# The memory tokens in four pieces, scaled by VectorE in the first layer

## The chip, the cores and the metric

The kernel runs on one core of one Trainium2 chip. The metric is the time of one execution in microseconds (us) of device time, the median of several runs. A profiled execution gives the trace from which rows are shown: PE is TensorE's matmul, PEld its weight load, DVE is VectorE, ACT ScalarE, POOL GpSimd, SP the engine that issues most copies; SPq, DVEq and so on are the engines' own instruction queues.

## The reference

The reference is a two-layer decoder trunk over 1024 tokens of width 1024 in float32. Each layer has a token mixer (a gated convolution in the first, attention with forget gates in the second), a cross-attention into 256 memory tokens with 4 heads, and a squared-ReLU MLP. What matters here is the memory side:

```
def memory_cross_attention(h, mem_n, w_q, w_k, w_v, w_o):
    q = (h @ w_q).reshape(B, S, MEM_HEADS, MEM_HEAD_DIM)
    k = (mem_n @ w_k).reshape(B, MEM_LEN, MEM_HEADS, MEM_HEAD_DIM)
    v = (mem_n @ w_v).reshape(B, MEM_LEN, MEM_HEADS, MEM_HEAD_DIM)
    ...
mem_n = rmsnorm(mem, norm_memsrc_g[l])
```

and the start of the convolution: `u = h @ w_pw1 + b_pw1`, with h = rmsnorm(x), then `a * sigmoid(gate)`, a depthwise convolution over 31 taps, and a layernorm over the width.

## The kernel before

The memory side is prepared ahead of its use. `memory_matrices`, a generator that is advanced a step at a time, multiplies wq with the keys and the values with wo, head by head, and stores the products (mqk, mvo) for later. It runs woven into `conv_layer`: a step for each half of x that is loaded, one behind each half that is normalized, two for each of the eight channel chunks of the convolution. A scheduler turns what the code issues into one fixed order for each engine; an engine takes its instructions in that order, and waits at one until what it needs is there. Instructions issued inside `tc.high_priority(offset=SMALL_FIRST)` are drawn forward in it.

The memory tokens lie in HBM with the width on partitions: `memT` is 128 x 8 chunks x 256 tokens, 1 MB. The steps of the first layer are these. One copy loads all of `mem`. ScalarE squares the eight chunks (L183 and L186, helper `sum_of_squares`), VectorE adds the squares (L187) into `acc`. TensorE multiplies `acc` with a column of 1/1024 (L162), VectorE adds epsilon (L210), GpSimd raises to the power -0.5 (L214), and TensorE spreads the result over the partitions (L171); VectorE keeps it as `mem_rs` (L483). ScalarE scales each chunk in place by the column `src0` of the gain (L471). The products of `mem` with two pieces of wk (tiles `praw`, 512 KB each, three buffers, L460) go into one PSUM bank of two halves of 8 products each (L276, helper `product`); VectorE multiplies that with `mem_rs` to get `kt` (L486). Products with two pieces of wv follow, copied out as `vt` by ScalarE (L488), then those of `kt` with wq, evacuated by ScalarE in quarters `o` (L503), then those of wo with `vt` (L521).

On the convolution's side the order is: `x` loaded in two halves of eight tiles of 256 KB (L135); squares of x, sums and inverse RMS by the same helpers; `h` (L225, VectorE), its high part (L229, ScalarE's cast) and low part (L149, VectorE), which together are `op`; the first gate weights split in the same way into `wh` (L152) and `wl` (L149); three products for each pair of parts (`op` with `wl`, and twice with `wh`); `u` (L390, VectorE); then the 49 instructions of VectorE per chunk that make the convolution (L413 to L428) and the sum `acc` for the layernorm (L361).

A product of two float32 operands stands in the trace as two MATMUL records, one of fp32r operands as one.

Of the kernel before, what the change touches and what calls it, by code (L numbers as in the profile page):

```python
# [12 lines left out]
F32 = mybir.dt.float32  # L13
F32R = mybir.dt.float32r
AF = mybir.ActivationFunctionType
ALU = mybir.AluOpType
# [3 lines left out]
P = 128  # L20
D = 1024
S = 1024
NCH = D // P
HALF = 512
MEM = 256
# [7 lines left out]
SMALL_FIRST = 4000  # L33
# [23 lines left out]
RMS_EPS = 1e-6  # L57
# [30 lines left out]
def trunk(ctx, tc, a, out):  # L88
    nc = tc.nc
    act, dve, pool, pe = nc.scalar, nc.vector, nc.gpsimd, nc.tensor  # L90
# [14 lines left out]
    def col(name, i):  # L105
        return par[:, COLS[name] + i : COLS[name] + i + 1]
# [31 lines left out]
    nrm = ctx.enter_context(tc.tile_pool(name="nrm", bufs=2))  # L138
# [3 lines left out]
    def bank(p):  # L142
        return p.tile([P, HALF], F32, name="mm", tag="mm")
# [11 lines left out]
    def token_mean(*accs):  # L155

        nb = accs[0].shape[-1] // P
        t = bank(ps)
        means = [t[:, i * nb : (i + 1) * nb] for i in range(len(accs))]
        for m, acc in zip(means, accs):  # L160
            for b in range(nb):
                pe.matmul(m[:, b : b + 1], acc[:, b * P : (b + 1) * P], mean_col, start=True, stop=True)  # L162
        return means

    def spread(v):

        nb = v.shape[-1]
        r = bank(ps)
        with tc.high_priority(offset=SMALL_FIRST):
            for b in range(nb):  # L170
                pe.matmul(  # L171
                    r[:, b * P : (b + 1) * P], v[:, b : b + 1].to_broadcast([P, P]), ident,
                    start=True, stop=True,
                )
        return r[:, : nb * P]

    def sum_of_squares(chunks):

        n = chunks[0].shape[-1]
        acc = nrm.tile([P, HALF], F32, name="acc", tag="t", bufs=4)[:, :n]  # L180
        for c, ch in enumerate(chunks):
            if c == 0:
                act.activation(acc, ch, AF.Square)  # L183
            else:
                sq = nrm.tile([P, HALF], F32, name="t", tag="t", bufs=4)[:, :n]
                act.activation(sq, ch, AF.Square)  # L186
                dve.tensor_tensor(acc, acc, sq, op=ALU.add)  # L187
        return acc
# [10 lines left out]
    def inverse_rms(chunks, eps):  # L199

        acc = sum_of_squares(chunks)
        with tc.high_priority(offset=SMALL_FIRST):
            return rms_of_sums([acc], eps)

    def rms_of_sums(accs, eps, name="r"):

        m, *rest = token_mean(*accs)
        nb = m.shape[-1]
        v = nrm.tile([P, 4], F32, name="v")[:, :nb]
        dve.tensor_scalar(v, m, eps, None, op0=ALU.add)  # L210
        for x in rest:
            dve.tensor_tensor(v, x, v, op=ALU.add)
        r = nrm.tile([P, 4], F32, name=name)[:, :nb]
        pool.tensor_tensor(r, v, mhalf[:, :nb], op=ALU.pow)  # L214
        return r
# [57 lines left out]
    def product(out_ps, terms):  # L273
        terms = [p for t in terms for p in passes(*t)]
        for i, (x, y) in enumerate(terms):
            pe.matmul(out_ps, x, y, start=i == 0, stop=i == len(terms) - 1)  # L276
# [176 lines left out]
    def memory_matrices(pp, pq, layer):  # L453

        wq, wk, wv, wo = (a[f"mem_{n}{layer}"] for n in ("wq", "wk", "wv", "wo"))
        ad, vd = mats[layer]

        def get(src):
            raw = pp.tile([P, NCH, P], F32, name="praw", bufs=3)
            nc.sync.dma_start(raw, src)  # L460
            return raw

        mem = pp.tile([P, NCH, MEM], F32, name="mem", bufs=1)
        nc.sync.dma_start(mem, a["memT"])
        if layer == 0:
            r = inverse_rms([mem[:, c, :] for c in range(NCH)], RMS_EPS)
            rt = const.tile([P, MEM // P], F32, name="mem_r")
            rs = const.tile([P, MEM], F32, name="mem_rs")
            mem_r.extend((rt, rs))
        for c in range(NCH):  # L470
            act.activation(mem[:, c, :], mem[:, c, :], AF.Copy, scale=col(f"src{layer}", c))  # L471
        for h in range(MEM_HEADS):
            kv = []
            for w, n in ((wk, "kt"), (wv, "vt")):
                t = bank(pq).rearrange("p (c m) -> p c m", c=2)
                for c in range(2):
                    x = get(w[2 * h + c])
                    product(t[:, c, :], [((x[:, k, :],), (mem[:, k, :],)) for k in range(NCH)])
                o = pp.tile([P, 2, MEM], F32, name=n, bufs=1)
                if w is wk:  # L480
                    if layer == h == 0:
                        dve.tensor_copy(rt, r)
                        dve.tensor_copy(rs, spread(r))  # L483
                    rb = mem_r[1].unsqueeze(1).to_broadcast([P, 2, MEM])
                    with tc.high_priority(offset=SMALL_FIRST):
                        dve.tensor_tensor(o, t, rb, op=ALU.mult)  # L486
                else:
                    act.copy(o, t)  # L488
                kv.append(o)
                yield  # L490
            kt, vt = kv
            for j in range(2):

                x = get(wq[h, j])
                for g in range(2):
                    t = bank(pq).rearrange("p (f m) -> p f m", f=2)
                    o = pp.tile([P, 4, P], F32, name="o").rearrange("p (f b) n -> p f (b n)", f=2)
                    for f in range(2):
                        product(t[:, f, :], [
                            ((x[:, 4 * c + 2 * g + f, :],), (kt[:, c, :],)) for c in range(2)  # L500
                        ])
                        gain = col(f"mem{layer}", 4 * j + 2 * g + f)
                        act.activation(o[:, f, :], t[:, f, :], AF.Copy, scale=gain)  # L503
                    nc.sync.dma_start(
                        ad[:, 4 * j + 2 * g : 4 * j + 2 * g + 2, h * MEM : (h + 1) * MEM], o
                    )
            yield
            for j in range(2):

                x = get(wo[h, j])  # L510
                for mc in range(2):
                    t = bank(pq)
                    product(t, [
                        (
                            (vt[:, c, mc * P : (mc + 1) * P],),
                            (x[:, 4 * c : 4 * c + 4, :].rearrange("p b n -> p (b n)"),),
                        )
                        for c in range(2)
                    ])
                    o = pp.tile([P, 4, P], F32, name="o")  # L520
                    act.activation(  # L521
                        o, t.rearrange("p (b n) -> p b n", b=4), AF.Copy,
                        scale=mem_r[0][:, mc : mc + 1],
                    )
                    nc.sync.dma_start(
                        vd[4 * j : 4 * j + 4, :, 2 * h + mc, :].rearrange("b p n -> p b n"), o
                    )
            yield
# [907 lines left out]
    with prep_pools(4) as pools, banks(2) as pm:  # L1436
        conv_layer(pm, chain(*(memory_matrices(*pools, l) for l in range(2))))
    sums = mem_attention(0)
# [90 lines left out]
```

## Time and profile before

| | us |
|---|---|
| median of 3 runs | 2794.61 |
| lowest, highest | 2787.88, 2794.71 |
| profiled execution | 2793.35 |
| its span, first to last instruction | 2791.6 |
| TensorE busy in it | 2722.8 |
| VectorE busy | 2019.9 |
| ScalarE busy | 1275.8 |

The span is the time between the first and the last instruction in the trace; the time of the same execution has 1.75 us around it. A row of a trace gives start, busy time, engine, line, operation, output and input tiles, shape and count of like instructions that follow each other; in brackets the idle time ahead and what ended it.

### The profile page before, as it was taken

What the parts mean: (1) busy time and instruction counts of PE and PEld (TensorE: products, weight loads), DVE (VectorE), ACT (ScalarE), POOL (GpSimd) and SP (SyncE); (2) the same over time, 40 slices, a digit from 0 to 9 for tenths busy, and PEclk for the clock granted to TensorE, in tenths of its full rate; (3) what the DMA queues carried; (4) which work ended last, traced back from release to release, by engine and by line L of the source; (5) the groups of instructions that cost most, each with busy time, mean ns of one, the idle gap of its engine ahead of it and who ended that gap; (6) DMA issues with size and microseconds to landing.
All of it is one profiled execution on the core that took longest, in us unless ns stands there. A gap on an engine that the chain in (4) does not pass through costs nothing. (4 is left out here: it accounts for less than half of the span.)

```text
span 2791.6 us, 35871 instructions
## 1 busy us (share of the span) xinstructions
PE 2722.8 (98%) x12840; PEld 2248.9 (81%) x12840; DVE 2019.9 (72%) x3118; ACT 1275.8 (46%) x2297; POOL 726.2 (26%) x489
## 2 busy tenths in 40 slices
PE   8999999999999999999999999999999999999998
PEld 6777777888888878888688888878888888878886
DVE  5999985555776667788787777775545866677886
ACT  5112134433365553334466666663423655543332
POOL 0000000000065633786000000000000365615773
PEclk9999999999999999999999999999999999999999
DMA  6334364420255576553222322244222355565651
GB/s 221 121 121 136 107 198 153 132 92 28 100 210 196 177 268 220 210 196 128 84 88 92 93 79 87 80 136 152 87 79 99 136 196 192 186 248 199 230 203 61
DMA packets 173426, 406.45 MB, mean 146 GB/s; under 512 B 18480, under 2 KB 47536, under 8 KB 172992
## 3 DMA queue, kind: packets, MB, share of 16 engines
q1 hardware_dynamic: 172992, 404.10, 42.8%
q8 instruction: 101, 1.65, 0.3%
q14 instruction: 77, 0.63, 0.1%
q10 hardware_dynamic: 256, 0.07, 0.0%
HBM read 280.75 MB, written 119.14 MB: 143 GB/s over the span
## 5 line engine op out<-in xcount | busy, mean ns | idle before, releaser
L1091 PE MATMUL mm<-op,w 128*128 128x512 f32 x5424 | 1237.6, 390 | 11.4 <-ACT m L975 8.3
L1091 PEld LDWEIGHTS mm<-op,w 128*128 128x128 f32 x5424 | 1020.3, 188 | 225.5 <-ACT m L975 9.2
L276 PE MATMUL mm<-op,wh 128*128 128x512 f32 x1056 | 329.3, 393 | 4.0 <-DVE op L149 3.9
L149 DVE TENSOR_TENSOR w<-r,w 128x512 fp32r<-128x512 f32 x264 | 275.0, 1045 | 32.7 <-ACT w L673 18.5
L673 ACT CAST w<-r 128x512 fp32r<-128x512 f32 x264 | 163.4, 622 | 265.4 <-PE mm L1091 237.7
L276 PEld LDWEIGHTS mm<-op,wh 128*128 128x128 f32 x1056 | 198.8, 189 | 49.2 <-DVE op L149 8.0
L1336 PE MATMUL mm<-op,wh 128*128 128x512 f32 x736 | 230.5, 394 | 0.0
L149 DVE TENSOR_TENSOR w<-t,w 128x512 fp32r<-128x512 f32 x180 | 196.5, 1106 | 31.9 <-ACT w L673 31.9
L276 PE MATMUL mm<-op,wl 128*128 128x512 f32 x528 | 209.8, 398 | 3.4 <-DVE wl L149 1.8
L667 POOL TENSOR_TENSOR t<-r,t 128x512 f32<-128x512 f32 x104 | 172.9, 1663 | 85.9 <-DVE w L149 81.6
L885 POOL TENSOR_TENSOR x<-x,x 128x512 f32<-128x512 f32 x112 | 165.0, 1496 | 112.5 <-ACT x L898 101.6
L214 POOL TENSOR_TENSOR r<-v,mhalf 128x4 f32<-128x4 f32 (+1 forms) x15 | 16.8, 1117 | 676.4 <-DVE v L210 665.4
L152 ACT CAST wh<-raw 128x1024 fp32r<-128x1024 f32 x96 | 100.7, 1050 | 194.9 <-PE mm L276 96.4
L673 ACT CAST w<-t 128x512 fp32r<-128x512 f32 x180 | 112.0, 622 | 153.8 <-PE mm L1091 118.0
L152 ACT CAST pth<-mm 128x512 fp32r<-128x512 f32 (+1 forms) x224 | 105.9, 496 | 149.4 <-PE mm L576 81.0
L987 DVE TENSOR_TENSOR x<-mm,x 128x512 f32<-128x512 f32 x160 | 109.3, 683 | 81.4 <-PE mm L1091 52.4
L1336 PEld LDWEIGHTS mm<-op,wh 128*128 128x128 f32 x736 | 138.6, 188 | 26.6
L1336 PE MATMUL mm<-op,wl 128*128 128x512 f32 x368 | 155.1, 421 | 2.9 <-DVE wl L149 1.9
L276 PE MATMUL mm<-op,xsh 128*128 128x512 f32 x512 | 157.8, 393 | 0.0
L428 DVE SCALAR_TENSOR_TENSOR x<-d,par,x 128x512 f32<-128x512 f32 x232 | 154.6, 745 | 0.0
L667 POOL TENSOR_TENSOR t<-r,r 128x512 f32<-128x512 f32 x52 | 80.0, 1539 | 280.2 <-DMA r<-in_ff_w 194.1
L149 DVE TENSOR_TENSOR wl<-raw,wh 128x1024 fp32r<-128x1024 f32 x96 | 116.7, 1222 | 38.2 <-ACT wh L152 36.4
(191 smaller groups left out, 4577.6 us busy)
## 6 DMA issues: line engine op xcount, KB each, us to landing
r<-in_ff_w SPq DMA_DIRECT2D x128, 512.0 KB, 4.1
op<-ua SPq DMA_DIRECT2D x80, 512.0 KB, 6.9
us<-x SPq DMA_DIRECT2D x128, 256.0 KB, 4.0
op<-us SPq DMA_DIRECT2D x64, 512.0 KB, 5.6
raw<-mvo SPq DMA_DIRECT2D x32, 512.0 KB, 3.3
ua<-ul SPq DMA_DIRECT2D x64, 256.0 KB, 2.7
ua<-uh SPq DMA_DIRECT2D x60, 256.0 KB, 2.7
raw<-in_pw SPq DMA_DIRECT2D x24, 512.0 KB, 5.1
```

Source lines behind the costliest of these rows:

```text
L149: dve.tensor_tensor(lo, src, hi.bitcast(F32), op=ALU.subtract)
L152: act.copy(hi, src)
L214: pool.tensor_tensor(r, v, mhalf[:, :nb], op=ALU.pow)
L276: pe.matmul(out_ps, x, y, start=i == 0, stop=i == len(terms) - 1)
L428: dve.scalar_tensor_tensor(out[s], d[:, j : j + n], w, y, op0=ALU.mult, op1=ALU.add)
L667: (dve if g in (2, 3, UP, UP + 1) else pool).tensor_tensor(t, raws[g, x], raws[g, y], op=ALU.subtract)
L673: act.copy(highs[n][0], raws[steps[n][:2]])
L885: eng.tensor_tensor(u[g, x], y1, y2, op=op_)
L987: dve.tensor_tensor(v, sums[key], v, op=ALU.add)
L1091: pe.matmul(sums[key], y, z, start=first and i == 0, stop=n == last_of[key] and i == len(terms) - 1, skip_group_check=True,)
L1336: pe.matmul(t, x, y, start=n == 0, stop=n == len(terms) - 1)
```

## The change

In the first layer `mem` is loaded by four copies of two chunks each, and the two pieces of wk are asked for among them: the first behind the first quarter, the second behind the last. ScalarE takes the eight squares alone. VectorE multiplies each chunk with its gain, in place, once ScalarE has squared it, and adds its square. The mean and the power are the same calls as before. In the second layer all stays as it was.

```
         mem = pp.tile([P, NCH, MEM], F32, name="mem", bufs=1)
-        nc.sync.dma_start(mem, a["memT"])
+        loaded_first = deque()
         if layer == 0:
-            r = inverse_rms([mem[:, c, :] for c in range(NCH)], RMS_EPS)
+
+            nc.sync.dma_start(mem[:, :2, :], a["memT"][:, :2, :])
+            loaded_first.append(get(wk[0]))
+            for c in range(2, NCH, 2):
+                nc.sync.dma_start(mem[:, c : c + 2, :], a["memT"][:, c : c + 2, :])
+            loaded_first.append(get(wk[1]))
+            sums = nrm.tile([P, HALF], F32, name="acc", tag="t", bufs=4)[:, :MEM]
+            for c in range(NCH):
+                sq = nrm.tile([P, HALF], F32, name="t", tag="t", bufs=4)[:, :MEM] if c else sums
+                act.activation(sq, mem[:, c, :], AF.Square)
+                dve.tensor_scalar(mem[:, c, :], mem[:, c, :], col("src0", c), None, op0=ALU.mult)
+                if c:
+                    dve.tensor_tensor(sums, sums, sq, op=ALU.add)
+            with tc.high_priority(offset=SMALL_FIRST):
+                r = rms_of_sums([sums], RMS_EPS)
             rt = const.tile([P, MEM // P], F32, name="mem_r")
             rs = const.tile([P, MEM], F32, name="mem_rs")
             mem_r.extend((rt, rs))
-        for c in range(NCH):
-            act.activation(mem[:, c, :], mem[:, c, :], AF.Copy, scale=col(f"src{layer}", c))
+        else:
+            nc.sync.dma_start(mem, a["memT"])
+            for c in range(NCH):
+                act.activation(mem[:, c, :], mem[:, c, :], AF.Copy, scale=col(f"src{layer}", c))
...
-                    x = get(w[2 * h + c])
+                    x = loaded_first.popleft() if loaded_first else get(w[2 * h + c])
```

The scheduler's order changes with it on every engine but GpSimd, from the start to the products of the first half of h with the first gate weights; from there on it is that of before. Three places are shown.

VectorE, from the first instruction that touches the memory tokens to the first low parts of h's work; before:

```order
L187 TENSOR_TENSOR acc<-acc,t 128x256 x7
L210 TENSOR_SCALAR v<-mm 128x2
L482 COPY mem_r<-r 128x2
L483 COPY mem_rs<-mm 128x256
L187 TENSOR_TENSOR acc<-acc,t 128x512 x7
L486 TENSOR_TENSOR kt<-mm,mem_rs 128x512
L210 TENSOR_SCALAR v<-mm 128x4
```

The same place of the change, from the last of the seven pairs of scale and add on:

```order
L476 TENSOR_SCALAR mem<-mem,par 128x256
L478 TENSOR_TENSOR acc<-acc,t 128x256
L210 TENSOR_SCALAR v<-mm 128x2
L498 COPY mem_r<-r 128x2
L499 COPY mem_rs<-mm 128x256
L187 TENSOR_TENSOR acc<-acc,t 128x512 x6
L502 TENSOR_TENSOR kt<-mm,mem_rs 128x512
L187 TENSOR_TENSOR acc<-acc,t 128x512
L210 TENSOR_SCALAR v<-mm 128x4
```

Seven adds have become eight scales and seven adds, and `kt` has moved ahead of the last add for the first half of x.

TensorE, from its first product to the products with the first gate weights; before:

```order
L276 MATMUL mm<-mem,praw 128x256 x2
L162 MATMUL mm<-mean_col,acc 128x1 x2
L276 MATMUL mm<-mem,praw 128x256
L171 MATMUL mm<-ident,r 128x128 x2
L276 MATMUL mm<-mem,praw 128x256 x14
L162 MATMUL mm<-mean_col,acc 128x1 x4
L276 MATMUL mm<-mem,praw 128x256 x2
L171 MATMUL mm<-ident,r 128x128 x4
L276 MATMUL mm<-mem,praw 128x256 x13
L276 MATMUL mm<-kt,praw 128x256 x12
L276 MATMUL mm<-op,wl 128x512
L276 MATMUL mm<-op,wh 128x512 x2
```

The same stretch of the change:

```order
L276 MATMUL mm<-mem,praw 128x256 x5
L162 MATMUL mm<-mean_col,acc 128x1 x2
L276 MATMUL mm<-mem,praw 128x256
L171 MATMUL mm<-ident,r 128x128 x2
L276 MATMUL mm<-mem,praw 128x256 x11
L162 MATMUL mm<-mean_col,acc 128x1 x4
L276 MATMUL mm<-mem,praw 128x256
L171 MATMUL mm<-ident,r 128x128 x4
L276 MATMUL mm<-mem,praw 128x256 x14
L276 MATMUL mm<-op,wl 128x512
L276 MATMUL mm<-op,wh 128x512
L276 MATMUL mm<-kt,praw 128x256 x12
```

Five products instead of two stand ahead of the mean of the memory tokens' squares, one instead of two between the mean and the spread for x, and a product of `op` with `wl` and one with `wh` have moved ahead of the products with `kt`.

ScalarE, from the casts of the first half of h to the first evacuations `o` of the products with `kt`; before:

```order
L229 CAST op<-h 128x512 x5
L488 COPY vt<-mm 128x512
L152 CAST wh<-raw 128x1024 x2
L229 CAST op<-h 128x512 x2
L503 ACTIVATE o<-mm,par 128x256 x2
L183 ACTIVATE acc<-x_78 128x512
```

The same place of the change:

```order
L229 CAST op<-h 128x512 x5
L504 COPY vt<-mm 128x512
L229 CAST op<-h 128x512
L152 CAST wh<-raw 128x1024
L229 CAST op<-h 128x512
L152 CAST wh<-raw 128x1024
L183 ACTIVATE acc<-x_78 128x512
L229 CAST op<-h 128x512
L186 ACTIVATE t<-x_80 128x512
L186 ACTIVATE t<-x_82 128x512
L186 ACTIVATE t<-x_84 128x512
L519 ACTIVATE o<-mm,par 128x256
```

A cast of h has moved between `vt` and the first `wh`, and the first evacuation `o` behind four squares of the second half of x.

## Rows read from the trace of the kernel before

**Rows 1.** The page: span, and busy time of the engines with their shares and numbers of instructions.

```profile
span 2791.6 us, 35871 instructions
...
PE 2722.8 (98%) x12840; PEld 2248.9 (81%) x12840; DVE 2019.9 (72%) x3118; ACT 1275.8 (46%) x2297; POOL 726.2 (26%) x489
```

**Rows 2.** Whom TensorE waited for in the first 60 us: us in total, times, longest.

```profile
PE mm L276 <- ACT mem L471: 8.7, 2, 8.3
PE mm L276 <- ACT o L503: 2.7, 2, 1.6
PE mm L171 <- POOL r L214: 1.2, 2, 0.8
```

**Rows 3.** Timeline, SyncE's copies and VectorE's first use of par. The copies from 6.24 on start when the copy eight places ahead of them has landed: mem at 6.24, the two pieces of wk at 7.54 and 8.84, the first tile of x at 9.52.

```profile
0.73 0.38 SPq L97 DMA_DIRECT2D par<-in_par  x1
...
3.19 0.17 DVE L401 COPY sums<-par 128x8 f32<-128x8 f32 x1 [1.87 <-DMA par<-in_par]
...
6.24 0.33 SPq L135 DMA_DIRECT2D x<-in_xT  x1
...
7.54 0.33 SPq L135 DMA_DIRECT2D x<-in_xT  x1
...
8.84 0.33 SPq L135 DMA_DIRECT2D x<-in_xT  x1
...
9.52 0.33 SPq L460 DMA_DIRECT2D praw<-in_mem_wv  x1
```

**Rows 4.** Timeline of ScalarE: the first square and the first scale.

```profile
6.24 0.42 ACT L183 ACTIVATE acc<-mem 128x256 f32<-128x256 f32 x1 [4.23 <-DMA mem<-in_memT]
...
7.79 0.49 ACT L471 ACTIVATE mem<-mem,par 128x256 f32<-128x256 f32 x1
```

**Rows 5.** The convolution: whom VectorE waited for from 75 to 390 us, whom TensorE waited for at L162 from 60 to 420 us (us in total, times, longest), and VectorE's row of `u` in its timeline.

```profile
DVE raw L263 <- DMA raw<-in_wk: 2.1, 1, 2.1
DVE kt L486 <- PE mm L276: 1.1, 1, 1.1
...
PE mm L162 <- DVE acc L361: 3.1, 1, 3.1
...
73.38 0.75 DVE L390 SCALAR_TENSOR_TENSOR u<-mm,par,sg 128x512 f32<-128x512 f32 x1 [2.55 <-PE mm L276]
```

**Rows 6.** Groups of VectorE's instructions by form: busy time, mean ns of one, idle time ahead.

```profile
L570 DVE TENSOR_SCALAR p<-p,rs 128x256 f32<-128x256 f32 x64 | 19.7, 350 | 0.9
```

**Rows 7.** Timeline of VectorE: the sum of the memory tokens' squares, `mem_rs`, and the adds for the first half of x.

```profile
7.00 3.61 DVE L187 TENSOR_TENSOR acc<-acc,t 128x256 f32<-128x256 f32 x7 [3.45 <-ACT t L186]
...
14.08 0.42 DVE L483 COPY mem_rs<-mm 128x256 f32<-128x256 f32 x1 [1.11 <-PE mm L171]
14.42 5.46 DVE L187 TENSOR_TENSOR acc<-acc,t 128x512 f32<-128x512 f32 x7
```

**Rows 8.** Timeline of TensorE in two stretches of products of mem with wk: start, busy time, number of records.

```profile
13.84 4.00 PE L276 MATMUL mm<-mem,praw 128*128 128x256 f32 x9
...
17.25 4.25 PE L276 MATMUL mm<-mem,praw 128*128 128x256 f32 x18
```

**Rows 9.** Timeline of VectorE and TensorE: `kt`, the mean of x's squares, and the first `h`.

```profile
21.54 0.69 DVE L486 TENSOR_TENSOR kt<-mm,mem_rs 128x512 f32<-128x512 f32 x1 [1.66 <-PE mm L276]
...
21.77 0.95 PE L162 MATMUL mm<-mean_col,acc 128*128 128x1 f32 x8
...
25.26 2.06 DVE L225 SCALAR_TENSOR_TENSOR h<-x,par,mm 128x512 f32<-128x512 f32 x3 [2.34 <-PE mm L171]
```

**Rows 10.** Timeline of ScalarE and VectorE around the first gate weights: `vt`, `wh`, `wl`, the last low part of the first half of h, an evacuation and a square, and the last add for the second half of x.

```profile
31.01 0.58 ACT L488 COPY vt<-mm 128x512 f32<-128x512 f32 x1
31.48 1.99 ACT L152 CAST wh<-raw 128x1024 fp32r<-128x1024 f32 x2
...
32.89 2.35 DVE L149 TENSOR_TENSOR wl<-raw,wh 128x1024 fp32r<-128x1024 f32 x2
...
37.62 0.69 DVE L149 TENSOR_TENSOR op<-h,op 128x512 fp32r<-128x512 f32 x1
...
41.72 0.47 ACT L503 ACTIVATE o<-mm,par 128x256 f32<-128x256 f32 x1 [1.12 <-DMA mqk<-o]
42.09 0.62 ACT L186 ACTIVATE t<-x 128x512 f32<-128x512 f32 x1
...
42.74 0.69 DVE L187 TENSOR_TENSOR acc<-acc,t 128x512 f32<-128x512 f32 x1 [0.42 <-ACT t L186]
```

**Rows 11.** TensorE: the last products of wv and the first of kt and the first products behind the spread for the second half of x, in the timeline; the products of the first half of `op` from 47.3 to 55.4 us (ns of one as min/median/max, first and last start); and the first product of praw with vt, in the timeline.

```profile
27.65 3.19 PE L276 MATMUL mm<-mem,praw 128*128 128x256 f32 x14
...
31.39 1.97 PE L276 MATMUL mm<-kt,praw 128*128 128x256 f32 x8 [0.55 <-DMA praw<-in_mem_wq]
...
47.37 0.71 PE L276 MATMUL mm<-op,wh 128*128 128x512 f32 x2
...
L276 PE MATMUL mm<-op,wh x24: 389/389/481, 47.4 to 55.2; 128*128 128x512 f32 x24
L276 PE MATMUL mm<-op,wl x11: 389/389/398, 47.9 to 54.7; 128*128 128x512 f32 x11
...
55.42 1.02 PE L276 MATMUL mm<-praw,vt 128*128 128x512 f32 x2
```

**Rows 12.** Busy time of the engines by stretch, with the granted clock of TensorE (PEclk), behind the pause at the end of the convolution.

```profile
389.70:396.50 6.80, 6.71 (x24) 6.08 (x25) 2.24 (x6) 1.19 (x3) 0.00 (x0) 0.50 0.07 8
```

## The prediction

> **What bounds the kernel now.** I read the page first: TensorE is busy for 2722.8 of 2791.6 us [rows 1], so it has about 69 us without work in the whole run, and nothing the change touches can win more than the part of these that lies beside it. The list of waits for the first 60 us comes next [rows 2]: TensorE stands 8.3 us before its first product, for a memory chunk that ScalarE has to scale, then 0.4 us for the next; after that 2.7 us for evacuations by ScalarE and 1.2 us for the inverse RMS. That is 12.6 us, nearly all that this stage could give.
>
> SyncE's rows show what is behind the 8.3 us [rows 3]. A copy that waits for an older one starts when that one has landed. So par landed at 3.19 (VectorE's first use), all of mem (1 MB) at 6.24, the first wk at 7.54, the second at 8.84, the first x at 9.52: the order of issue, one after the other. The first weights were there 0.8 us before the first product; in those 0.8 us ScalarE finished squares and the first scale [rows 4].
>
> What comes behind must be looked at before a gain is booked. During the convolution VectorE sets the time: from 75 to 390 us it waits 3.2 us in all, and TensorE at the end waits 3.1 us for VectorE's last sum [rows 5]. VectorE starts that long chain on u, when TensorE has done the second half of the first gate product (73.38). So the quantity to work out is how much earlier or later TensorE comes to that point.
>
> **The first product.** The landings are moved only within the same bytes. mem's first quarter should land 3.05 / 4 = 0.76 us after par, at 3.95 (3.05 us is mem behind par), wk 1.30 us later at 5.25, the other quarters, at the 0.68 us of an x tile of the same 256 KB, at 5.9, 6.6 and 7.3, and the second wk at 8.6 to 8.8, as before. ScalarE squares chunk 0 in 0.42 (4.4); VectorE scales it. The trace has such a scale, with a column of numbers and in place: 0.35 us [rows 6]. Chunk 0 is ready at 4.8, wk later, so the first product starts at 5.3, 3.0 us sooner. That is the gain at the door. Its bounds: if pieces are no faster than the whole, 7.55 (0.8 sooner); never before 4.8.
>
> The Trainium skill speaks against this change: "DMA: Bandwidth & Descriptors", section Bandwidth, wants copies batched to 1 MiB or more and has 138 GB/s for 64 KB beside 341 for 1 MB. The row of x says 256 KB in 0.68 us, 385 GB/s, where copies stand in a queue, against 344 for the 1 MB of mem, so the trace of this kernel does not bear it out. By 138 GB/s (an estimate from that page of the Trainium skill) four pieces would take 7.6 us instead of 3.05, the last land at 12.1, and the sum below would be +4.5.
>
> **The mean of the squares.** VectorE now does eight scales and seven adds where it did seven adds (one per 0.53 us, as ScalarE and the running sum allow). A pair of scale and add costs 0.27 + 0.34 = 0.61 us if the next instruction starts 0.08 before the end of the last, as 14.08 + 0.42 and 14.42 show [rows 7], and 0.78 if it doesn't. From 6.4 (chunk 2 squared) six pairs end at 10.15 (or 11.1), against 10.6 before. So this chain gains 0.45 us at best, though its data come sooner: it has become VectorE's. TensorE has five products issued before it (two before), waits for it, does one more, waits for the power, and spreads: next product at 13.4 instead of 13.84, with 10 products of wk left instead of 13.
>
> **What a product costs there** depends on TensorE's clock. Nine records from 13.84 take 4.00 us, 18 from 17.25 take 4.25 us [rows 8]: 0.43 us a step, then 0.215, the 1.2 and the 2.4 GHz levels, the second after a stretch of products without a pause. The page's granted clock doesn't show the early level, so I go by the spacing. A product is two records. If the level rises again only after the spreading, at 16.6 to 20, the tenth product ends at 19.3 to 21.2; if it is high from 13.4, at 17.9. Before: 21.5.
>
> **Order takes it back, first place.** VectorE's `kt` now stands ahead of the seventh add of x. The six adds end at 18.65 (0.45 sooner start; 0.79 each, seven in 5.46 before [rows 7]); kt then waits for the tenth product. With the low level kt runs at 19.4 to 21.3, the add 0.62 behind it, and the mean of x is multiplied at 21.0 to 22.8 instead of 21.77 [rows 9]; with the high level at 20.15. Call the shift of h's first row (25.26) d: between -0.8 and +1.0, or -1.6 with the high level. I take -0.1, as the low level, near the middle of its bounds, is the likelier. The loads of the second half of x come sooner too, since the eighth product frees the queue ahead of them, but nobody waits for them then.
>
> **Second place: the hole.** Behind the 16 wv products TensorE went on at once with products of kt and wq (31.39) and came to op and wl when these were long made. Now two products of op stand ahead of the kt products, the first with wl. Times from here are plus d. One more wv product is left, so vt is copied at 31.45, not 31.01 [rows 10]. Behind it ScalarE casts one h (to 32.55), then wh, 1.05 us, to 33.5; VectorE makes wl in 1.22 us, to 34.75. TensorE ended at 31.3: it stands still for 3.5 us. Four kt products follow to 37.0, then a second hole: the first evacuation now stands on ScalarE behind two squares, of which the second waits until VectorE has made the last low part (37.75; 38.3 before). Square 38.4, evacuation 38.8; products resume 1.8 us later. From there squares (0.62) and evacuations (0.47) take turns; the seventh add ends at 43.1 (43.43 before), the spread at 46.4 (47.37 before).
>
> At 47.37 before had 35 products of op left, 0.23 us each [rows 11], and was through at 55.42. Now at 46.4, 43 of op and 4 of kt are left: 43 x 0.23 + 4 x 0.43 = 11.6, so 58.0. That is **+2.6 + d**. The second half of h comes sooner than TensorE needs it, and everything behind 58 is in the order of before, so this shift is carried to 73.38 and through VectorE's chain to the end.
>
> **The sum.** +2.6 - 0.1 = +2.5 us. Bounds: with the high level +1.0; with d = +1.0, +3.6; and the 3.5 us hole may cost TensorE its clock, as after the hole of 3.1 us at the end of the convolution, behind which 6.8 us ran at half [rows 5, 12]: only some 1.2 us of that would come through, the rest lies in the second hole. So +1 to +4.8. The profiled run took 2793.35, its span and 1.75 around it; 2793.35 + 2.5 = 2795.9. The profiled run lies 1.3 below the median of 2794.61, and the runs spread over 6.8 us. Some 0.3%, 8.4 us, is what can be told from no change; both the gain at the door and the loss behind it are below it.
>
> A second rule of the Trainium skill, "VectorE: DVE Perf Modes", section "The DRAIN you can't avoid", says that the next instruction does not start until the pipe is empty, which would give 0.78 a pair, the mean 0.95 later and a sum of +3.4. The row at 14.42 shows the overlap here, and I go by it.
>
> **Rivals.** *The gain at the door stays* (0.21): for this the kt products must not be held, that is, wl must be there when wv ends. The row of 32.89 speaks against it, since wh waits for vt on ScalarE in both orders. Time: 2793.35 - 3.0 = 2790.3. *The change doesn't do what it says* (0.09): the pieces share the queue so badly that the first product starts little sooner and the last piece later than mem did. par, 188 KB, took 2.45 us from its issue to 3.19; pieces of that cost would land at 5.6, then wk 6.9, and 9.4, 11.8, 14.3, the mean at 15.5 instead of 10.6. Then six adds of x end at 24.0, kt and the seventh at 25.3, d is +3.7, and the time 2793.35 + 2.6 + 3.7 = 2799.7. The rows of x, 0.68 us each, are against it. The Trainium skill's rule on batching above is on its side. *Slower beyond the 0.3%* (0.04): the clock falls in the hole and stays at the lower level until 58. Then 43 products cost 0.43, not 0.23: +8.6 + 2.5, 2804.4. It decides from 30 such products on; the row after 389.7 shows a return after 6.8 us, which speaks against it. Faster by over 0.3% (0.03) would need 8.4 us of the 12.6 us above, which I can't find. The forecast has the rest, 0.63, with 2794 to 2798.5 as its own range.
>
> **How the numbers follow.** Faster 0.03, same 0.92, slower 0.05 (the slow rival and a little beside it). The range has to take in the second case (2790.3), the third (2799.7), and the spread of the runs: 2788.5 to 2800.5.
>
> **What would show it.** First product at 5.3; VectorE's fifteen instructions ending near 10.15; TensorE's first wq product near 35 and a wait of over 3 us for wl ahead of it; the praw, vt products starting at 57 to 59, not 55.42; u at 75 to 77; a wait for VectorE at the end of the convolution still there. Wrong if u comes before 73.4: then the hole is smaller than ScalarE's rows make it, or the clock rose early; or if the convolution ends otherwise than u says, so that VectorE doesn't carry the shift.

## The result and the profile after

The changed kernel takes 2799.43 us (median of 11 runs, 2796.09 to 2804.11), the kernel before 2792.87 us (11 runs, 2787.88 to 2797.05): a ratio of 1.0024, 95% interval 1.0016 to 1.0032. That is within 0.3%, but it is a loss of about 6.5 us, where the sum of the prediction had 2.5. The profiled execution took 2799.39, its span is 2797.6.

The page's span and busy times, to be read against [rows 1]: TensorE has 3 us more of busy time and 6 us more of span.

```profile
span 2797.6 us, 35878 instructions
...
PE 2726.0 (97%) x12840; PEld 2250.0 (80%) x12840; DVE 2018.8 (72%) x3126; ACT 1273.2 (46%) x2289; POOL 726.7 (26%) x489
```

Whom TensorE waited for in the first 60 us (us in total, times, longest), to be read against [rows 2]:

```profile
PE mm L276 <- DMA praw<-in_mem_wk: 7.3, 1, 7.3
PE mm L276 <- DVE wl L149: 3.4, 1, 3.4
PE mm L162 <- DVE acc L187: 1.6, 1, 1.6
PE mm L171 <- POOL r L214: 1.6, 3, 0.8
PE mm L162 <- DVE acc L478: 0.5, 1, 0.5
```

The door is gained by one microsecond only, 7.3 for 8.3, and it is now the weights that are late, not the scaled tokens. Even that is a good execution: three others with these loads and this scaling (e1, e6 and e10 below) have their first product at 7.83 to 7.96, and six with the one copy and ScalarE's scaling (before, e2, e5, e7, e9, e11) at 8.03 to 8.53, so that the gain is some 0.6 us on average. The evacuations (2.7 us) are gone from the list. In their place stand 3.4 us for wl and 1.6 us for the seventh add of x.

SyncE's copies, each of which starts when the one eight places ahead has landed (as in [rows 3]): here wk at 7.19, the second memory quarter at 8.57, the last at 9.88, the second wk at 11.21.

```profile
7.19 0.33 SPq L135 DMA_DIRECT2D x<-in_xT  x1
...
8.57 0.33 SPq L135 DMA_DIRECT2D x<-in_xT  x1
...
9.88 0.33 SPq L135 DMA_DIRECT2D x<-in_xT  x1
...
11.21 0.33 SPq L135 DMA_DIRECT2D x<-in_xT  x1
```

TensorE's timeline (start, busy time, records; idle time ahead in brackets), to be read against [rows 9, 11]: the mean of x, the spread for the first half of x, the hole at wl, the kt products, mean and spread for the second half, and the first product on vt.

```profile
21.51 1.05 PE L162 MATMUL mm<-mean_col,acc 128*128 128x1 f32 x8 [1.63 <-DVE acc L187]
...
23.90 2.07 PE L171 MATMUL mm<-ident,r 128*128 128x128 f32 x8 [0.28 <-POOL r L214]
...
37.07 0.79 PE L276 MATMUL mm<-op,wl 128*128 128x512 f32 x1 [3.40 <-DVE wl L149]
...
38.09 7.70 PE L276 MATMUL mm<-kt,praw 128*128 128x256 f32 x24
...
45.88 1.05 PE L162 MATMUL mm<-mean_col,acc 128*128 128x1 f32 x8
...
48.35 1.16 PE L171 MATMUL mm<-ident,r 128*128 128x128 f32 x8 [0.83 <-POOL r L214]
...
60.89 1.45 PE L276 MATMUL mm<-praw,vt 128*128 128x512 f32 x3
```

The second spread of the kernel before, which the rows above do not show, and VectorE's row of `u` in the changed kernel, to be read against [rows 5]:

```profile
46.45 1.16 PE L171 MATMUL mm<-ident,r 128*128 128x128 f32 x8 [0.84 <-POOL r L214]
```

```profile
78.85 0.75 DVE L390 SCALAR_TENSOR_TENSOR u<-mm,par,sg 128x512 f32<-128x512 f32 x1 [2.55 <-PE mm L276]
```

Two numbers sum it up. The second spread starts at 48.35; before it was at 46.45, so it is 1.90 later. From it to the first product on vt TensorE now needs 12.54 us without a pause, before 8.97: 3.57 more. Together that is 5.47, and u comes at 78.85 instead of 73.38, the same 5.47 later.

The stretches of TensorE's granted clock (PEclk, the third number from the end), which [rows 12] show for the kernel before only at 390 us: 0.50 of full speed, the 1.2 GHz level, in two stretches, one behind the wait for the seventh add and one behind most of the hole. The kernel before stands at 1.00 from 20 to 60 us.

```profile
20.00:22.40 2.40, 0.89 (x8) 0.93 (x9) 1.36 (x3) 0.00 (x0) 0.00 (x0) 0.99 1.00 349
22.40:29.20 6.80, 6.52 (x21) 5.08 (x21) 3.35 (x7) 1.85 (x3) 1.01 (x1) 0.50 0.89 349
29.20:36.00 6.80, 4.47 (x21) 3.60 (x19) 5.42 (x10) 3.53 (x6) 0.00 (x0) 1.00 0.41 131
36.00:42.80 6.80, 5.73 (x14) 4.54 (x15) 6.49 (x9) 5.91 (x11) 0.00 (x0) 0.50 0.53 181
```

### The profile page after: what moved, and what is told of

The parts are those of the page before. It is cut to its first block, busy times and chain, and to the rows that moved or that the text cites. A ratio compares the mean times of both kernels' runs of the same rounds, so it can differ in the third digit from the quotient of the medians.

```text
span 2797.6 us, 35878 instructions
## 1 busy us (share of the span) xinstructions
PE 2726.0 (97%) x12840; PEld 2250.0 (80%) x12840; DVE 2018.8 (72%) x3126; ACT 1273.2 (46%) x2289; POOL 726.7 (26%) x489
```

## The experiments

Three theories. **Order**: the loss is the new order, wl's product ahead of the kt products and kt ahead of the seventh add. **Loading**: it is the late landing of the pieces. **Clock**: it is the two stretches at half speed, whatever the order. Each experiment has a 95% interval against the kernel before. In the table, times are starts in each profiled execution; "behind" is the time from the second spread to the product on vt. No experiment leaves any of the computation out.

| kernel | first h | second spread | vt product | behind | ratio |
|---|---|---|---|---|---|
| before | 25.26 | 46.45 | 55.42 | 8.97 | |
| changed | 26.02 | 48.35 | 60.89 | 12.54 | 1.0024 [1.0016, 1.0032] |
| e1 changed, old order | 26.17 | 48.16 | 57.14 | 8.98 | 1.0009 [1.0000, 1.0018] |
| e2 before, new order | 25.86 | 47.59 | 60.13 | 12.54 | 1.0027 [1.0018, 1.0036] |
| e3 VectorE scaling | 24.50 | 46.21 | 55.18 | 8.97 | 1.0001 [0.9993, 1.0010] |
| e4 pieces | 26.51 | 47.72 | 56.70 | 8.98 | 1.0008 [0.9999, 1.0017] |
| e5 = e2, filler too long | 27.59 | 50.84 | 63.38 | 12.54 | 1.0026 [1.0015, 1.0037] |
| e6 = changed, filler too long | 28.71 | 49.88 | 62.41 | 12.53 | 1.0030 [1.0020, 1.0039] |
| e7 two products ahead | 25.36 | 48.93 | 57.89 | 8.96 | 1.0005 [0.9997, 1.0014] |
| e8 weights first, old order | 23.58 | 44.10 | 53.05 | 8.95 | 1.0006 [0.9998, 1.0015] |
| e9 = e2, filler to size | 25.68 | 46.50 | 60.71 | 14.21 | 1.0032 [1.0020, 1.0044] |
| e10 = changed, filler to size | 26.34 | 46.74 | 59.27 | 12.53 | 1.0017 [1.0009, 1.0026] |
| e11 kt ahead | 26.99 | 48.60 | 57.57 | 8.97 | 1.0005 [0.9996, 1.0014] |
| e12 weights first, own order | 24.83 | 45.16 | 59.37 | 14.21 | 1.0010 [1.0001, 1.0018] |

The column "behind" divides the kernels cleanly: 8.95 to 8.98 in the old order, 12.53 or 12.54 in the new one (14.21 where half speed falls into it).

**e1 and e2: order against loads.** A helper chains named instructions of each engine, without waits of its own; the lists are those of the other kernel.

```diff
+    def follow(orders):
+        at = {i.name: i for i in nc.cur_bb.bb.instructions}
+        for names in orders:
+            for a, b in zip(names, names[1:]):
+                tc.add_manual_dep(
...
         conv_layer(pm, chain(*(memory_matrices(*pools, l) for l in range(2))))
+        follow(ORDERS)
```

> The changed kernel with its loads and its scaling as they are, but from the x adds on every engine's instructions (TensorE, VectorE, ScalarE, SyncE, up to about 75 us) chained in the order that they had in the kernel before; nothing else differs. Theory 'order' (the loss is the new order: the gated unit's first wl product ahead of the kt products, and kt ahead of the seventh x add): the hole of 3.4 us behind wl is gone, the first product on vt starts at 54.5 to 56.5 us (55.42 before, 60.89 changed) and the time is back within 1.5 us of the kernel before, 2792 to 2794.5. Theory 'loading' (the loss is that the memory quarters and the weights land late: second wk at 11.19 instead of 8.82 us, x some 2.3 us later): the products on vt stay at 59 us or later and the time at 2797.5 to 2800. Theory 'clock' (the two falls of TensorE's clock at 22.36 and 36.02 us are the loss, whatever the order): if a fall before 60 us is still in the clock records the time stays above 2796, if none is there it is that of 'order'.

> The reverse: the kernel before with one copy of the memory tokens and ScalarE's scaling, but from the x adds on every engine's instructions chained in the order that they have in the changed kernel. 'order': the hole behind wl is there (3 to 4 us at about 33 us), the products on vt start at 58 to 61 us and the time is 2797 to 2799.5. 'loading': it stays within 1.5 us of the kernel before, 2791.5 to 2794.3. 'clock': the hole alone costs the 2.6 us of the prediction (about 2795.5) if the clock records show no fall before 60 us, and the whole loss (2798 to 2799.5) only if they do.

e2, which has none of the change but its order, takes 2798.05 us and the whole loss. e1, which has all of the change but its order, loses 0.09%, with an interval that ends at no loss. TensorE in e2 (the helper moves line numbers up by 16):

```profile
35.36 0.50 PE L292 MATMUL mm<-op,wl 128*128 128x512 f32 x1 [3.49 <-DVE wl L165]
...
45.23 0.95 PE L178 MATMUL mm<-mean_col,acc 128*128 128x1 f32 x8
...
47.59 1.16 PE L187 MATMUL mm<-ident,r 128*128 128x128 f32 x8 [0.84 <-POOL r L230]
...
60.13 2.31 PE L292 MATMUL mm<-praw,vt 128*128 128x512 f32 x5
```

The hole is there with the old loads, and 12.54 us of work behind the spread. So 'order' holds and 'loading' falls as the main cause. It is a smaller part, though: e1 has its vt product 1.72 us later than before, a little beyond the 56.5 expected. The two kernels' delays, 4.71 and 1.72, add up to more than the 5.47 of the whole change, so they are not shares of one sum.

'Clock', whatever the order, falls as well. e1 has two stretches of half speed before 60 us, for which that theory had a time above 2796, and took 2794.33:

```profile
23.20:26.60 3.40, 3.40 (x13) 2.61 (x12) 0.43 (x1) 0.00 (x0) 0.80 (x1) 0.50 1.03 389
...
36.80:40.20 3.40, 3.40 (x10) 2.69 (x9) 2.52 (x5) 2.74 (x7) 0.00 (x0) 0.50 0.81 287
```

The chaining itself costs nothing that shows: e3 below is chained too and stands at 1.0001.

**e3 and e4: the two halves of the change, each in the old order.** e3 has one copy (`nc.sync.dma_start(mem, a["memT"])` in place of the pieces), e4 the pieces with the old squares and scalings:

```diff
-            for c in range(NCH):
-                sq = nrm.tile([P, HALF], F32, name="t", tag="t", bufs=4)[:, :MEM] if c else sums
-                act.activation(sq, mem[:, c, :], AF.Square)
-                dve.tensor_scalar(mem[:, c, :], mem[:, c, :], col("src0", c), None, op0=ALU.mult)
...
+            r = inverse_rms([mem[:, c, :] for c in range(NCH)], RMS_EPS)
```

> One copy of the memory tokens as in the kernel before, VectorE's scaling and adds beside ScalarE's squares as in the changed kernel, and the order of the kernel before from the x adds on. The scaling alone: the pairs take 0.60 us each from about 6.7, so the sum of squares ends near 11.4 instead of 10.60 us, and the first product waits for wk (7.53) instead of the scaled tokens (8.33). 'order' and 'loading' both give 2791.5 to 2794.5 (no change); a loss of 2 us or more would say that VectorE's adds or scalings themselves are the cost, which neither says.

> Four pieces with the weights between them as in the changed kernel, but squares and scalings on ScalarE as in the kernel before, and the order of the kernel before from the x adds on. ScalarE has sixteen operations to do and the last quarter lands at about 9.9 instead of 6.2 us, so its own squares end some 1.5 to 3 us later and x is squared that much later. 'order': the second product group absorbs it, 2792.5 to 2795.5. 'loading': the delay of 2.3 us or more comes through to the products on vt (58 us or later) and to the end, 2795.5 to 2799.

VectorE's scaling alone changes nothing (vt 0.24 us sooner, ratio 1.0001). The pieces alone put the vt product 1.28 us later and cost 0.08%, with an interval that just takes in zero. So what the loads cost lies with the pieces, not with the scaling; but this is a reading of single executions, of which e1 and e3 have two stretches of half speed before 60 us and e4 has none, so that 1.28 and 0.24 us are no exact prices.

**e8: where the pieces lose.** The share of time in which the DMA engines worked (last but one) and the GB/s (last), by microsecond, in the changed kernel:

```profile
3.50:4.50 1.00, 0.00 (x0) 0.00 (x0) 0.03 (x1) 0.00 (x0) 0.00 (x0) 1.00 0.44 150
4.50:5.50 1.00, 0.00 (x0) 0.00 (x0) 0.44 (x2) 0.72 (x2) 0.00 (x0) 1.00 0.77 236
```

and in the kernel before:

```profile
3.50:4.50 1.00, 0.00 (x0) 0.00 (x0) 0.05 (x1) 0.00 (x0) 0.00 (x0) 1.00 1.00 418
```

Behind the first quarter the engines move little until the weights flow. In the other executions with these loads the same microsecond has 182 GB/s (e1), 178 (e4), 168 (e6) and 102 (e10), but shares from 0.62 to 0.84, so that it isn't shown whether the engines stand idle there or work slowly. e8 turns these two round, in the old order:

```diff
-            nc.sync.dma_start(mem[:, :2, :], a["memT"][:, :2, :])
             loaded_first.append(get(wk[0]))
+            nc.sync.dma_start(mem[:, :2, :], a["memT"][:, :2, :])
```

> The changed kernel with the first weights (512 KB) issued ahead of the four memory pieces instead of behind the first of them, and the order of the kernel before from the x adds on (as e1). If the gap of the DMA engines between 3.3 and 5.2 us in the changed kernel comes from a short copy (256 KB) running out before the next one has begun, it is gone or under 0.3 us here: weights at 4.7 to 5.1, first memory quarter at 5.4 to 5.9, first product at 5.7 to 6.4 instead of 7.96 us (e1), second weights at 8.9 to 9.4 instead of 11.2; h at 24.3 to 25.3, vt at 54.5 to 56, time 2790.5 to 2793.5. If pieces are slow wherever they stand, the second weights stay at 10.5 or later, the first product at 7 or later and the time at that of e1 (2794.3).

That holds in part. The same microsecond in e8:

```profile
3.50:4.50 1.00, 0.00 (x0) 0.00 (x0) 0.14 (x1) 0.00 (x0) 0.00 (x0) 1.00 0.86 244
```

and in its timeline TensorE's first product, the landing of the second wk on SyncE (9.87 for 11.21; 8.84 before), and the first product on vt:

```profile
7.45 3.84 PE L292 MATMUL mm<-mem,praw 128*128 128x256 f32 x10 [7.45 <-DVE mem L492]
...
9.87 0.33 SPq L151 DMA_DIRECT2D x<-in_xT  x1
...
53.05 7.03 PE L292 MATMUL mm<-praw,vt 128*128 128x512 f32 x16
```

The loss of rate is smaller, but not gone; the pieces still move fewer GB/s than the one copy. The first product at 7.45 misses the 5.7 to 6.4 expected. Yet the vt product is 2.37 us sooner than before, the best of all, and the time still no better than before (1.0006). Nor is this gain the loads' alone: against e1, which has the same order, the first product is 0.51 us sooner and the vt product 4.09, and e8 has neither of e1's stretches of half speed (its spread for the first half of x takes 1.16 us, e1's 2.08).

**e7 and e11: the two swaps of the order, each alone in the kernel before.** e7 moves the gated unit's first two products ahead of the kt products in TensorE's list, e11 moves kt ahead of the seventh add in VectorE's (the numbers are instructions, `...` stands for those left out):

```diff
 # e7, TensorE's list
-    ... 216, 325, 326, ..., 355, 363, 364, 365 ...
+    ... 216, 363, 364, 325, 326, ..., 355, 365 ...
 # e11, VectorE's list
-    ... 271, 274, 187, 281 ...
+    ... 271, 187, 274, 281 ...
```

> The kernel before, all engines in its own order, but for TensorE's first two products of the gated unit (on wl and wh), which stand ahead of the twelve kt products as in the changed kernel. VectorE has wl ready at 34.11 us, so a wait of some 2.8 us from 31.3 us takes the place of waits of 0.55 and 1.59 us. 'order', told apart further: if this swap is the whole of it, the products on vt start 3 to 5 us later (58.4 to 60.4) and the time is 2794.5 to 2797; if it takes the later casts and wl subtractions on ScalarE and VectorE as well, vt is 0 to 1.5 us later (55.4 to 57) and the time 2791 to 2793.5. With a fall of the clock near 33 us in the records the first is the likelier.

> The kernel before, all engines in its own order, but for one instruction on VectorE: kt's multiplication stands ahead of the seventh add of x's squares, as in the changed kernel. kt takes 0.69 us, needs the second pair of products on wk and was waited for by nobody before 31.4 us. By the prediction's first place the mean of x follows the seventh add at once, so h starts 0 to 0.9 us later than 25.26 and the products on vt 0 to 0.9 us later than 55.42, time 2790.5 to 2793.5. If this swap is a large part of the new order's cost (e2's 4.7 us less e7's 2.5), vt is 1.5 us or more later.

```profile
34.26 0.50 PE L292 MATMUL mm<-op,wl 128*128 128x512 f32 x1 [3.32 <-DVE wl L165]
...
48.93 1.16 PE L187 MATMUL mm<-ident,r 128*128 128x128 f32 x8 [0.84 <-POOL r L230]
```

So e7 has the hole, and its vt product is 2.47 us later, between the two cases expected; half speed falls into it from 34.7 to 38.1. But the work behind the spread is that of before: for the other 2.2 us of e2 the rest of the order is needed. In e11:

```profile
22.50 1.02 PE L178 MATMUL mm<-mean_col,acc 128*128 128x1 f32 x8 [1.04 <-DVE acc L203]
...
24.88 2.08 PE L187 MATMUL mm<-ident,r 128*128 128x128 f32 x8
```

The mean comes 0.73 later, by kt's 0.69 us, as was said. But TensorE has waited 1.04 us for it, half speed follows (the spread takes 2.08, not 1.16), and h is 1.73 later, twice the bound. The vt product is 2.15 later. That 2.47 and 2.15 add up to nearly the 4.71 of e2 doesn't explain e2: it has none of e11's half speed ahead of h, and the 3.57 behind its spread are in neither swap. Neither swap shows in the time by itself.

**e5, e6, e9, e10: the clock.** Products that nobody reads fill TensorE's waits, in e2 and in the changed kernel:

```diff
+            def filler(n):
+                t = bank(ps)
+                for _ in range(n):
+                    pe.matmul(t[:, :256], ident, par[:, :256], start=True, stop=True)
```

> The kernel before in the changed kernel's order (as e2_before_in_new_order) with one addition: sixteen products of the identity with the parameters (128x256, their result is read by nobody) stand on TensorE between the last product on the memory tokens and the gated unit's first product on wl, where e2 waited 3.49 us; at the high level they should take about 16 x 0.215 = 3.4 us and hide in the wait. If the clock is part of the loss: no fall near 36.75 us in the records, the 24 kt products take about 5.7 instead of 8.6 us, the products on vt start at 57.3 to 58.4 instead of 60.13 us, and the time is 2 to 3 us below that of e2, 2795 to 2796.5. If only the idle time of the new order counts: vt at 59.8 to 60.5 and 2797.5 to 2799, as e2.

> The changed kernel with its loads, scaling and order, and only such filler products added on TensorE whose result nobody reads: seven (1.5 us) ahead of the mean of x, where it waited 1.63 us for the seventh add, and sixteen (3.4 us) ahead of the first wl product, where it waited 3.40 us. If the clock is part of the loss: neither fall (22.36 and 36.02 us) is there, the 28 products from 25.8 us take 6.2 instead of 7.9 us, the kt products 5.7 instead of 7.7 us, vt at 57 to 58.5 instead of 60.89, and the time 2795 to 2797 instead of 2799.4. If only idle time counts: vt at 60.5 to 61.2, time 2798.5 to 2800.5.

I had sized them wrong: each is two records, so that the sixteen took 7.07 us and not 3.4, and they made both kernels later. They say nothing on the clock's share.

> As e5_hole_filled, with half the filler: one of these products is two records of 0.22 us, so that the sixteen of e5 took 7.07 us and ran 3.6 us past the wait that they were to fill. Eight should take 3.5 us, the length of the wait for wl in e2 (3.49). If the clock is part of the loss: no fall near 36 us in the records, the 24 kt products in 5.4 us (as e5: 5.35) where e2 took 8.6, the products on vt at 57.3 to 58.5 instead of 60.13 us, the time some 2 us below that of e2 (2795 to 2797). If only idle time counts: vt at 59.8 to 60.5, time 2797 to 2799.

> As e6_changed_waits_filled, with fillers of the length of the waits: three products (1.3 us) ahead of the mean of x and eight (3.5 us) ahead of the first wl product; e6 had twice that and more. If the clock is part of the loss: neither fall of the changed kernel before 60 us (22.36 and 36.02) is there, the 28 products on the memory tokens take 6.2 instead of 7.9 us and the kt products 5.4 instead of 7.7, vt at 57 to 58.8 instead of 60.89, time 2795 to 2797.5. If only idle time counts: vt at 60.5 to 61.3, time 2798.5 to 2800.

e10, fillers included:

```profile
32.19 3.62 PE L357 MATMUL mm<-par,ident 128*128 128x256 f32 x16
...
36.42 1.89 PE L292 MATMUL mm<-kt,praw 128*128 128x256 f32 x8
39.86 3.74 PE L292 MATMUL mm<-kt,praw 128*128 128x256 f32 x16 [1.55 <-ACT o L544]
...
44.31 1.02 PE L178 MATMUL mm<-mean_col,acc 128*128 128x1 f32 x8 [0.48 <-DVE acc L203]
...
46.74 1.16 PE L187 MATMUL mm<-ident,r 128*128 128x128 f32 x8 [0.84 <-POOL r L230]
...
59.27 3.17 PE L292 MATMUL mm<-praw,vt 128*128 128x512 f32 x7
```

With 5.1 us of work added (3.62 here and 1.46 ahead of the mean of x), the same instructions in the same order reach vt 1.62 us sooner than in the changed kernel, between the two cases expected, though h is 0.32 later. Both stretches of half speed are gone: the kt products take 5.63 us, not 7.70. What remains against the kernel before is 0.29 at the spread, in which the loads and the fillers have a part, and 3.56 behind it, the work that the order has moved there. The intervals of the times, 1.0017 and 1.0024, overlap, so for the whole run this is a direction and not a proof. And e9 shows the limit:

```profile
46.50 2.04 PE L187 MATMUL mm<-ident,r 128*128 128x128 f32 x8 [0.83 <-POOL r L230]
...
60.71 1.88 PE L292 MATMUL mm<-praw,vt 128*128 128x512 f32 x4
```

The hole no longer costs the clock, the spread comes 1.09 sooner than in e2, and then half speed falls on the spread and what follows (14.21 us for 12.54): vt is no sooner than in e2, and later than both ranges expected.

**e12: better loads without the order.** e8's loads, nothing chained.

> The changed kernel with only the first weights issued ahead of the four pieces (the loads of e8), nothing chained: the scheduler's own order, which again has the first wl product ahead of the kt products. 'order': the loads are as in e8 (first product near 7.4, second weights near 9.9 us), but a wait of 3 us or more for wl is there and the products on vt start 3 to 5 us later than in e8 (53.05), at 56 to 58, time 2794 to 2797. 'loading': with the better order of the loads the loss is gone, vt at 53 to 55 and time 2791 to 2793.5.

```profile
34.33 0.50 PE L276 MATMUL mm<-op,wl 128*128 128x512 f32 x1 [3.92 <-DVE wl L149]
...
45.16 1.92 PE L171 MATMUL mm<-ident,r 128*128 128x128 f32 x8 [0.83 <-POOL r L214]
...
59.37 3.16 PE L276 MATMUL mm<-praw,vt 128*128 128x512 f32 x7
```

The spread is 1.29 us sooner than before, and the vt product 3.95 later. The order takes back more than the loads give; 1.0010, as 'order' expected, though vt is 6.3 us later than in e8, not 3 to 5 (1.7 of that is half speed behind the spread).

## Why the prediction was right, and where it was not

The forecast, no change that 0.3% can tell, and the place of the loss were right; the size, +2.5 us for +6.5, was not. The time of 2799.43 lies in the stated range, which had been widened for a rival at 2799.7, and not in the forecast's own 2794 to 2798.5; vt (57 to 59) and u (75 to 77) were missed too, at 60.89 and 78.85. That the time comes so near to that rival's is luck: it had d at +3.7 and 2.6 us behind it, and the runs have d at +0.76 and the rest behind it.

**First product**, 5.3 predicted, 7.31 measured, near the late bound. The step that failed here is the landing of wk: 5.25 predicted by bytes in a full queue, 7.19 measured. I took the queue to stay full behind the small first copy, and the DMA engines moved 150 GB/s from 3.5 to 4.5 us, for 418 before. The Trainium skill's rule on batches, "DMA: Bandwidth & Descriptors", section Bandwidth, speaks for the sign, and this trace agrees that the pieces land late. Not with its price: the quarters behind wk follow one another in 0.65 us each (8.57 to 9.88 is two). The rival "the change doesn't do what it says" is thus half true: e4 shows 1.28 us of it.

**Mean of squares.** A pair takes 0.60 us, as predicted (0.61): in the timeline VectorE's scales start at 9.03 and 9.63. By the rule that was quoted from "The DRAIN you can't avoid" in "VectorE: DVE Perf Modes" of the Trainium skill it would be 0.78; the same section adds that a next instruction which is not held starts earlier, and with that the 0.60 agrees. But the last quarters came 2.6 us later than I had them, so the sum ended at 12.71, not 10.15.

**First place.** The mean of x at 21.51 lies in the 21.0 to 22.8 predicted, and d is +0.76, inside its bounds, not the -0.1 chosen. But that is luck: two errors cancel. The six adds ended at 20.16 and not at 18.65, since the sum of squares was late, and `kt` followed them without a wait:

```profile
15.50 4.66 DVE L187 TENSOR_TENSOR acc<-acc,t 128x512 f32<-128x512 f32 x6
20.08 0.69 DVE L502 TENSOR_TENSOR kt<-mm,mem_rs 128x512 f32<-128x512 f32 x1
```

The low level, on which d was chosen, wasn't there either: 22 records behind the spread, from 14.96 us, took 4.91 us, 0.22 each, so that `kt` waited for no product.

**Second place.** The hole is 3.40 us for 3.5 predicted, for the reason given: ScalarE copies vt, casts one h and then wh, and VectorE makes wl.

```profile
33.71 0.58 ACT L504 COPY vt<-mm 128x512 f32<-128x512 f32 x1 [1.86 <-PE mm L276]
34.19 0.62 ACT L229 CAST op<-h 128x512 fp32r<-128x512 f32 x1
34.71 1.05 ACT L152 CAST wh<-raw 128x1024 fp32r<-128x1024 f32 x1
...
35.79 1.23 DVE L149 TENSOR_TENSOR wl<-raw,wh 128x1024 fp32r<-128x1024 f32 x1 [0.25 <-ACT wh L152]
```

This chain starts when the last wv product ends, so no gain ahead of it can shorten the hole; e12, with better loads, has 3.92. The second hole, 1.8 us, is there in e10 (1.55) and not in the changed kernel, where the kt products at half speed fill it. The work left behind the spread was right too: 8 more products of op and 4 of kt, 8 x 0.23 + 4 x 0.43 = 3.56, and 3.57 was measured. With d put in, 58.0 + 1.08 = 59.1 for e10, which measured 59.27.

**The clock** is the step that failed. I let the hole cost at most 1.2 us of it, and saw no other wait that could. The fall behind the hole did stay mostly hidden: the mean at 45.88 follows the seventh add, which ended at 45.83, and lies 12.17 us behind the start of vt's copy, in e10, without the fall, 11.92. (In e2 it is 13.33, in e9 12.34: there the fall costs 1 us.) But the 1.63 us for the seventh add, which the first place makes and which I did not book as a wait, has half speed behind it. The wv products in the changed kernel and in e10:

```profile
25.77 7.90 PE L276 MATMUL mm<-mem,praw 128*128 128x256 f32 x28
```

```profile
26.14 6.21 PE L292 MATMUL mm<-mem,praw 128*128 128x256 f32 x28
```

vt's copy then starts at 33.71, 2.70 later than [rows 10], and the hole, wl and the seventh add (45.83 for 43.1) move with it. 58.0 + 0.76 = 58.8 was to be had by my own steps; 60.89 is 2.1 above it, and e10 gives back 1.62 of it. e10 fills both waits at once; that the first gives back most of this is read from the rows (vt's copy 1.32 us sooner), not tested by itself.

**Carried through.** As said: u is 5.47 later, and VectorE's instructions at 300 us are 5.7 later. The total is another matter: the medians of the thirteen kernels lie on average 1.3 us above the shift of their own profile at u, with a scatter of 1.5, e8 even 3.8 above (-2.4 at u, +1.4 in the median), e11 2 below. Between u and the end stand waits at which the clock falls in one execution and not in another: at the end of the convolution for 6.8 us before, not at all in e8 and e10. Why the gain of e8 is not in its median stays open.

**The rivals.** "The gain at the door stays" fell, by the hole that was argued against it. "The clock stays low until 58" fell: it was back after 6.8 us each time.

## What to carry to other kernels

Where a scheduler orders the program, compare the orders first: a change of the loads of one tile moved a product of the convolution's side to a place where its operand was not yet made, and that order alone, put on the unchanged kernel, cost as much as the whole change. Chaining each kernel in the other's order tells the two apart. Count what work is left behind the last point where another engine sets the time: what the order moves behind that point comes back in full, here 3.57 us for 3.56 added up. And price a new wait on TensorE twice, for itself and for the half speed that may follow, here behind waits of 1.0 to 1.6 us.

## What the runs showed of the hardware

- Behind a 256 KB copy near the head of the queue the next copy was slow to flow: 102 to 182 GB/s from 3.5 to 4.5 us in five executions (changed, e1, e4, e6, e10), against 385 to 418 in seven with 1 MB in its place (before, e2, e3, e5, e7, e9, e11) and 244 and 211 in two with 512 KB there and the quarters behind (e8, e12). The second wk, behind the same bytes, landed at 11.21 (changed), 8.84 (before) and 9.87 (e8). Why is open.
- Half speed came behind waits of TensorE of 1.0 us (e11, from 23.8 us), 1.2 us (e1, from 23.2 us) and 1.6 us, not only of 3. A wait of that size doesn't always bring it: e2 and e8 have 1.04 and 1.23 us at the same place and keep the higher level there. Work that nobody reads kept the clock up where it filled a wait (e10), and did not save it from the next one (e9).
